# Which engine subtracts the low parts of the mixer's weights

## The chip, the core and the metric

The kernel runs on one core of a Trainium2 chip as one program. Its time is the device time of one execution in microseconds (us). The five engines of the core work side by side and each takes its instructions strictly in the order in which they were written when the program was built: TensorE (PE, matrix products), VectorE (DVE), ScalarE (ACT), GpSimd (POOL) and SyncE (SP, which here issues DMAs). What one engine needs of another it waits for on semaphores.

## The reference

The reference computes two blocks of a language model in float32 for one sequence of 512 frames with 1024 channels. The first block is a hybrid mixer followed by a convolutional feed-forward net; the second has two layers, each a mixer (stick-breaking attention with pooling, then gated linear attention) and a feed-forward net. The change lies in the first mixer. Cut to what matters there:

```
h = rms_norm(x, pre_mix_norm)
proj = h @ w_in                                   # 1024 x 6688
qkv = silu(causal_dwconv(q, k, v))                # gated delta rule, 8 heads
o_a = gdn_chunked(l2norm(q), l2norm(k), v, g, beta)   # per chunk a triangular solve,
                                                  # then a recurrence over the chunks
o_a = rms_norm(o_a) * silu(z_a)
xbc = silu(causal_dwconv(x_s, b_s, c_s))          # Mamba-2 state space, 16 heads
y = rms_norm((ssd_chunked(xbc, dt, ...) + d * x_s) * silu(z_s))
x = x + rms_norm(concat(o_a, y) @ w_out, post_mix_norm)
```

## The kernel before

All activations lie with channels on the 128 partitions and the 512 frames along the free axis. A weight matrix is read in tiles of 128 x 1024 floats. For accuracy close to float32 each weight tile and each activation is kept as two parts in a rounded format: a high part, which is a cast, and a low part, which is the original minus the high part. One product then takes three matmuls: high times high (L214), high weight times low activation (L215), low weight times high activation (L216).

A weight tile goes through `wload`: SP issues the DMA into `wr` (two buffers), ACT casts `wr` to `wh` (L202), and a subtraction makes `wl` (L205). `wh` and `wl` have four buffers each. In the first mixer (`mix1`, which sets `s.wpool = WP` at L611 and back to 0 at L1051) the subtraction of every second tile is on GpSimd and that of the others on VectorE:

```
        s.nw += 1
        e = nc.gpsimd if s.wpool and s.nw % s.wpool == 0 else nc.vector
        e.tensor_tensor(lo[:, :f], raw[:, :f], hi[:, :f], ALU.subtract)
```

`mix1` treats the eight heads of the gated delta rule in four pairs (`gdn`). For each pair, TensorE makes the products of keys (L747) and of keys with queries (L769), DVE masks and scales them, a reduction (L756) collects the diagonal blocks, which go through DRAM and back (L757, L762) to lie as the solve needs them. The solve itself is a chain of thirty small DVE instructions (L791, L792, each needing the one before), ended by two L801. After it TensorE transposes the result (`pX`, L798), two levels of block inversion follow (L812 to L836), then the recurrence over four chunks (L851 to L867), the norm (a chain L183 to L188, then L877) and a transpose into place (`pfo`, L880). In the text, a *solve* is the stretch from the second L756 of a pair to its first L801.

Beside this, projections are fed to TensorE as filling: those of the next pair of heads (L474, L479, L691 are their convolution and activation), of the gates, and of the state-space part (`xbc`). Which filling stands between which steps of the chain, and in which order each engine sees its instructions, is settled when the program is built by a scheduler, which goes by priorities and by its own estimate of how long each instruction takes. The state-space part (`ssd_prep`, `ssd_core`) transposes its inputs (`ps`, L698), scales them on DVE (L957) and GpSimd (L960, `xd`), and accumulates states (`pS`, L971) and outputs (`py`, L999; `pf`, L1022). GpSimd also makes a mask product per head (L771), some low parts of activations (L296), and issues the loads of decay rows (L677).

Of the kernel before, what the change touches and what calls it, by code (L numbers as in the profile page):

```python
# [90 lines left out]
class Prog:  # L91
# [513 lines left out]
    def mix1(s, after):  # L605
# [4 lines left out]

        s.wpool = WP  # L611
        rv = s.cp.tile([P, 64], F32, name="rv")
# [795 lines left out]
GF = [[0], [1], [2, 3], []]  # L1408
PA = 0
PB_ = 2  # L1410
WP = 2
EO = (0, 1, 0, 4, 4, 4, 1, 6, 6, 6, 6, 4, 2, 5, 5, 2, 5, 3, 5, 3)
HE = 0
FA = 13
# [153 lines left out]
```

## Time and profile before

| | |
|---|---|
| median of 3 runs | 2156.12 us (2152.16 to 2157.94) |
| the profiled execution, own time | 2157.26 us |
| its span, first to last instruction | 2155.3 us |
| TensorE busy in the span | 2083.8 us (97%) |
| VectorE busy | 1392.2 us (65%) |
| ScalarE busy | 944.4 us (44%) |
| GpSimd busy | 152.0 us (7%) |
| mean granted TensorE clock | 0.984 |

The first mixer takes about the first 620 us of the span. Busy time counts instructions from start to end, so a DVE instruction that started and was then held up counts as busy. A row of a timeline gives the start in the span, the duration, the engine, the line of the kernel, the operation, what it writes and reads, and in brackets how long the engine stood idle before it and what ended that idle time.

### The profile page before, as it was taken

Reading aid. Unit: us, or ns where it says so; the run is one execution under the profiler, and the core shown is the slowest. Engines: PE = TensorE matmul, PEld = TensorE weight load, DVE = VectorE, ACT = ScalarE, POOL = GpSimd, SP = SyncE. Lnnn points to the kernel's source line nnn. Section 1 sums busy time; section 2 is a strip of 40 time slices with the busy share of each in tenths; the row PEclk is TensorE's granted clock in tenths of the full one; section 3 lists DMA queues with packets and bytes.
Section 4 is the critical chain, followed back from the end, with each engine's and each line's share of the span. In section 5 each row is a group of like instructions: output and inputs, shape, how many; then the busy total and the mean of one; then the engine's idle time right before and its main releaser. Section 6 shows DMA issues by size and latency. Waiting matters only on the chain.

```text
span 2155.3 us, 27129 instructions
## 1 busy us (share of the span) xinstructions
PE 2083.8 (97%) x10558; PEld 1740.6 (81%) x10558; DVE 1392.2 (65%) x2353; ACT 944.4 (44%) x1557; POOL 152.0 (7%) x109
## 2 busy tenths in 40 slices
PE   8989989988999999999999999999999999999999
PEld 7777878877788888889777788888889888888887
DVE  6868666687579777227887787763243576777621
ACT  6434435356455444224765444442242434444311
POOL 1111111134000000000000100001000001000000
PEclk9999999999999999999999999999999999999999
DMA  4213131233213223332212132233322122322331
GB/s 163 96 54 97 40 98 52 69 108 98 97 51 119 98 96 96 98 101 80 67 47 66 55 121 95 97 94 97 94 81 88 59 79 68 118 98 98 95 116 64
DMA packets 60358, 189.16 MB, mean 88 GB/s; under 512 B 7901, under 2 KB 13277, under 8 KB 60230
## 3 DMA queue, kind: packets, MB, share of 16 engines
q1 hardware_dynamic: 57874, 180.75, 26.1%
q0 software_dynamic: 2032, 6.59, 0.9%
q8 instruction: 83, 1.36, 0.2%
q14 instruction: 45, 0.37, 0.0%
q10 hardware_dynamic: 324, 0.09, 0.0%
HBM read 184.99 MB, written 2.41 MB: 87 GB/s over the span
## 4 chain that ended last, share of the span: by engine, by line
PE 80%; DVE 11%; ACT 4%; DMA 2%; issue 2%; POOL 1%; SPq 0%; ACTq 0%; POOLq 0%; DVEq 0%
PE pp L214 23%; PE pp L216 23%; PE pp L215 23%; DVE qkv L479 1%; DVE wl L205 1%; DMA wr<-in_w_qkvz 1%; PE pT L812 1%; PE pz L1124 1%; PE pU L819 1%; DVE xbc L479 1%; PE pS L1367 1%; ACT wh L202 1%; PE po L1376 1%; DVE s L791 1%; DVE t L683 1%
## 5 line engine op out<-in xcount | busy, mean ns | idle before, releaser
L214 PE MATMUL pp<-a,wh 128*128 128x512 f32 (+1 forms) x2128 | 825.5, 389 | 8.5 <-ACT a L295 2.5
L215 PE MATMUL pp<-a,wh 128*128 128x512 f32 (+1 forms) x2128 | 819.7, 386 | 2.8 <-POOL a L296 2.2
L216 PE MATMUL pp<-a,wl 128*128 128x512 f32 (+1 forms) x2128 | 818.9, 385 | 3.3 <-POOL wl L205 1.7
L202 ACT CAST wh<-wr 128x1024 fp32r<-128x1024 f32 (+3 forms) x327 | 336.2, 1030 | 512.9 <-PE pp L215 370.0
L205 DVE TENSOR_TENSOR wl<-wr,wh 128x1024 fp32r<-128x1024 f32 (+2 forms) x297 | 358.1, 1206 | 235.9 <-ACT wh L202 232.2
L214 PEld LDWEIGHTS pp<-a,wh 128*128 128x128 f32 x2128 | 403.3, 190 | 92.7 <-issue 8.3
L215 PEld LDWEIGHTS pp<-a,wh 128*128 128x128 f32 x2128 | 404.0, 190 | 82.5 <-issue 4.0
L216 PEld LDWEIGHTS pp<-a,wl 128*128 128x128 f32 x2128 | 403.7, 190 | 81.5 <-DVE wl L205 2.9
L466 DVE TENSOR_TENSOR u<-pp,rb 128x512 f32<-128x512 f32 x198 | 135.6, 687 | 172.2 <-PE pp L216 170.7
L479 DVE SCALAR_TENSOR_TENSOR c<-u,pv,c 128x511 f32<-128x511 f32 (+1 forms) x264 | 196.3, 747 | 3.9
L216 PE MATMUL pp<-t,wl 128*128 128x512 f32 (+1 forms) x336 | 130.9, 389 | 0.0
L214 PE MATMUL pp<-t,wh 128*128 128x512 f32 (+1 forms) x336 | 130.7, 389 | 0.0
L215 PE MATMUL pp<-t,wh 128*128 128x512 f32 (+1 forms) x336 | 129.7, 386 | 0.0
L214 PE MATMUL pp<-wh,a 128*128 128x256 f32 (+2 forms) x384 | 112.6, 295 | 6.4 <-ACT wh L355 4.9
L215 PE MATMUL pp<-wl,a 128*128 128x256 f32 (+2 forms) x384 | 112.6, 293 | 0.0
L216 PE MATMUL pp<-wh,a 128*128 128x256 f32 (+2 forms) x384 | 112.6, 293 | 0.0
L476 ACT ACTIVATE c<-u,pv 128x512 f32<-128x512 f32 x132 | 107.5, 815 | 10.8 <-DVE u L466 10.3
L205 POOL TENSOR_TENSOR wl<-wr,wh 128x1024 fp32r<-128x1024 f32 x30 | 73.8, 2462 | 353.3 <-ACT wh L202 252.3
L499 ACT ACTIVATE c<-c 128x512 f32<-128x512 f32 x66 | 41.7, 632 | 106.7 <-DVE c L479 106.4
L214 PEld LDWEIGHTS pp<-wh,a 128*128 128x128 f32 x384 | 74.3, 194 | 8.4 <-ACT wh L355 4.9
L315 POOL TENSOR_TENSOR t<-t,t 128x512 f32<-128x512 f32 x18 | 29.4, 1635 | 727.6 <-ACT t L313 727.2
L295 ACT CAST t<-c 128x512 fp32r<-128x512 f32 x42 | 26.1, 621 | 114.9 <-DVE c L500 114.9
(343 smaller groups left out, 2353.0 us busy)
## 6 DMA issues: line engine op xcount, KB each, us to landing
wr<-in_w_up SPq DMA_DIRECT2D x132, 512.0 KB
wr<-in_w_dn SPq DMA_DIRECT2D x48, 448.0 KB
wr<-in_w_qkvz SPq DMA_DIRECT2D x32, 512.0 KB
wr<-in_w_dn SPq DMA_DIRECT2D x24, 512.0 KB
t<-gcd POOLq DMA_DIRECT2D x24, 256.0 KB, 4.4
wr<-in_w_xbc SPq DMA_DIRECT2D x12, 512.0 KB
a<-bdd SPq DMA_DIRECT2D x32, 128.0 KB
wr<-in_w_o1a SPq DMA_DIRECT2D x8, 512.0 KB
```

Source lines behind the costliest of these rows:

```text
L202: nc.scalar.copy(hi[:, :f], raw[:, :f])
L205: e.tensor_tensor(lo[:, :f], raw[:, :f], hi[:, :f], ALU.subtract)
L214: mm(out, l[0], r[0], start=first, stop=False)
L215: mm(out, l[0], r[1], start=False, stop=False)
L216: mm(out, l[1], r[0], start=False, stop=last)
L295: nc.scalar.copy(hi, src)
L315: (nc.vector if s.pool_sq or last else nc.gpsimd).tensor_tensor(s.acc, s.acc, sq, ALU.add)
L466: s.nc.vector.tensor_tensor(u, ps, rb, ALU.mult)
L476: nc.scalar.activation(c, u, AF.Identity, scale=w(taps - 1), bias=bias)
L479: nc.vector.scalar_tensor_tensor(c[:, sh:], u[:, :S - sh], w(j), c[:, sh:], ALU.mult, ALU.add)
L499: nc.scalar.activation(g, g, AF.Silu)
L683: v.tensor_scalar(r[:, c * P:(c + 1) * P], r[:, c * P:(c + 1) * P], gc3[:, c, h:h + 1], 0.0, ALU.subtract, ALU.min)
```

## The change

The constant that chooses which tiles of the first mixer go to GpSimd goes from 2 (every second) to 0 (none).

```
-WP = 2
+WP = 0
```

All else of the source stays. The scheduler, however, now has 30 instructions fewer on GpSimd and 30 more on DVE, and it lays out all engines anew for the stretch of the first mixer; after that stretch the order is as before. On GpSimd, from the program's start to the first mask products (L771), the piece of the difference reads:

```order
-L205 ISA
-L205 TENSOR_TENSOR wl_496<-wr_493,wh_495 128x1024
-L205 TENSOR_TENSOR wl_574<-wr_571,wh_573 128x1024
 L677 DMA t_610<-gcd 128x512
 L677 DMA t_612<-gcd 128x512
-L205 TENSOR_TENSOR wl_819<-wr_816,wh_818 128x1024
-L205 TENSOR_TENSOR wl_948<-wr_945,wh_947 128x1024
+L771 ISA
 L771 TENSOR_TENSOR t_610<-t_610,cmix_281 128x512
```

All subtractions are gone, and the loads of decay rows and the mask products stand behind nothing but each other. On DVE, in the middle of the first pair's solve, this stood before (`s_894`, `s_896` are the running solution and a product; `u` and `qkv` belong to a projection of the next heads):

```order
L791 TENSOR_TENSOR s_896<-a_718,s_894 128x8x12
L205 TENSOR_TENSOR wl_1103<-wr_1100,wh_1102 128x1024
L792 TENSOR_TENSOR s_894<-s_894,s_896 128x8x12
L791 TENSOR_TENSOR s_896<-a_719,s_894 128x8x11
L466 TENSOR_TENSOR u_1015<-pp_990,rb_364 128x512
L792 TENSOR_TENSOR s_894<-s_894,s_896 128x8x11
L791 TENSOR_TENSOR s_896<-a_719,s_894 128x8x10
L792 TENSOR_TENSOR s_894<-s_894,s_896 128x8x10
L791 TENSOR_TENSOR s_896<-a_719,s_894 128x8x9
```

and this stands now:

```order
L791 TENSOR_TENSOR s_896<-a_719,s_894 128x8x11
L205 TENSOR_TENSOR wl_1103<-wr_1100,wh_1102 128x1024
L792 TENSOR_TENSOR s_894<-s_894,s_896 128x8x11
L466 TENSOR_TENSOR u_1015<-pp_990,rb_364 128x512
L791 TENSOR_TENSOR s_896<-a_719,s_894 128x8x10
L205 TENSOR_TENSOR wl_1137<-wr_1134,wh_1136 128x1024
L792 TENSOR_TENSOR s_894<-s_894,s_896 128x8x10
L479 SCALAR_TENSOR_TENSOR qkv_1017<-u_1015,pv,qkv_1017 128x511
L791 TENSOR_TENSOR s_896<-a_719,s_894 128x8x9
```

The tile `wl_1137`, which GpSimd subtracted before, now stands between two links of the chain, beside `wl_1103`. On TensorE, at the start of the state-space part, this stood before (the transposes `ps`, then filling `pp`, then the states `pS`):

```order
L698 MATMUL ps_4018<-cst,xbc_3933 128x128 x4
L214 MATMUL pp_4298<-a_126,wh_4294 128x512
...
L214 MATMUL pp_4298<-a_218,wh_4294 128x512
L698 MATMUL ps_4029<-cst,xbc_3972 128x128 x4
L971 MATMUL pS_4040<-xd_4002,Bt_3982 128x128
L971 MATMUL pS_4040<-xd_4013,Bt_3982 128x128
L971 MATMUL pS_4040<-xd_4024,Bt_3982 128x128
```

and this stands now:

```order
L880 MATMUL pfo_3737<-cst,t_3735 128x128 x4
L698 MATMUL ps_3983<-cst,xbc_3777 128x128 x4
L945 MATMUL pc_3989<-xbc_3816,xbc_3777 128x128 x4
...
L698 MATMUL ps_4029<-cst,xbc_3972 128x128 x4
L214 MATMUL pp_4337<-a_218,wh_4333 128x512
L215 MATMUL pp_4337<-a_219,wh_4333 128x512
L971 MATMUL pS_4040<-xd_4002,Bt_3982 128x128
L216 MATMUL pp_4337<-a_218,wl_4334 128x512
```

Before, 39 matmuls of filling stood between the last `pfo` of the heads and the first of these transposes, and 16 between the transposes and the states; now the transposes follow `pfo` at once and the states come after two matmuls of filling.

## Rows read from the trace of the kernel before

**Rows 1.** Busy time per engine, granted clock (PEclk): the first mixer, and a half-clock stretch
```profile
0.00:620.00 620.00, 561.90 (x3260) 484.92 (x3260) 441.07 (x944) 294.15 (x650) 111.48 (x82) 0.95 0.27 88
207.80:221.50 13.70, 12.87 (x52) 11.49 (x52) 6.92 (x9) 3.76 (x6) 2.54 (x1) 0.50 0.25 78
```

**Rows 2.** TensorE's waits in the first mixer: us in total, times, longest
```profile
PE pX L798 <- DVE t L801: 22.6, 4, 8.7
PE pf L1022 <- ACT a L1019: 6.5, 2, 4.0
...
PE pfo L880 <- DVE t L877: 2.8, 3, 2.3
PE po L459 <- DVE t L455: 2.5, 1, 2.5
PE pp L215 <- POOL a L296: 2.2, 2, 1.4
...
PE pp L216 <- POOL wl L205: 1.7, 1, 1.7
```

**Rows 3.** TensorE at the transposes behind the four solves
```profile
117.44 1.11 PE L798 MATMUL pX<-cst,t 128*128 128x128 f32 x4 [6.82 <-DVE t L801]
208.59 1.11 PE L798 MATMUL pX<-cst,t 128*128 128x128 f32 x4 [4.48 <-DVE t L801]
299.06 1.12 PE L798 MATMUL pX<-cst,t 128*128 128x128 f32 x4 [8.75 <-DVE t L801]
380.93 0.66 PE L798 MATMUL pX<-cst,t 128*128 128x128 f32 x4 [2.56 <-DVE t L801]
```

**Rows 4.** The subtractions on each engine, first mixer: busy, mean ns, idle before
```profile
L205 POOL TENSOR_TENSOR wl<-wr,wh 128x1024 fp32r<-128x1024 f32 x30 | 73.8, 2462 | 353.3 <-ACT wh L202 252.3 <-PE pp L216 26.4 <-DVE s L187 25.6
L205 DVE TENSOR_TENSOR wl<-wr,wh 128x1024 fp32r<-128x1024 f32 x40 | 50.9, 1273 | 21.7 <-ACT wh L202 21.3 <-issue 0.3
```

**Rows 5.** GpSimd in the first solve
```profile
101.67 2.39 POOL L205 TENSOR_TENSOR wl<-wr,wh 128x1024 fp32r<-128x1024 f32 x1 [13.10 <-ACT wh L202]
110.15 2.35 POOL L205 TENSOR_TENSOR wl<-wr,wh 128x1024 fp32r<-128x1024 f32 x1 [6.09 <-ACT wh L202]
```

**Rows 6.** DVE in the first solve
```profile
86.92 2.19 DVE L479 SCALAR_TENSOR_TENSOR qkv<-u,pv,qkv 128x509 f32<-128x509 f32 x1
...
99.09 0.74 DVE L479 SCALAR_TENSOR_TENSOR qkv<-u,pv,qkv 128x509 f32<-128x509 f32 x1
...
101.80 2.37 DVE L791 TENSOR_TENSOR s<-a,s 128x88 f32<-128x88 f32 x1
...
110.15 0.68 DVE L466 TENSOR_TENSOR u<-pp,rb 128x512 f32<-128x512 f32 x1
110.75 1.81 DVE L791 TENSOR_TENSOR s<-a,s 128x48 f32<-128x48 f32 x1
```

**Rows 7.** DVE at other places: two norms, the third and the fourth solve
```profile
26.25 2.22 DVE L186 TENSOR_TENSOR s<-R 128x4 f32<-128x4 f32 x1
...
157.59 0.16 DVE L186 TENSOR_TENSOR s<-s 128x8 f32<-128x8 f32 x1
157.78 2.35 DVE L187 SCALAR_TENSOR_TENSOR s<-s,s 128x8 f32<-128x8 f32 x1
...
290.30 1.23 DVE L205 TENSOR_TENSOR wl<-wr,wh 128x1024 fp32r<-128x1024 f32 x1 [3.55 <-ACT wh L202]
...
366.08 0.28 DVE L791 TENSOR_TENSOR s<-a,s 128x120 f32<-128x120 f32 x1 [4.15 <-DMA a<-bdd]
...
374.23 2.42 DVE L791 TENSOR_TENSOR s<-a,s 128x48 f32<-128x48 f32 x1
```

**Rows 8.** TensorE's pace on filling, six matmuls apart
```profile
480.65 0.39 PE L214 MATMUL pp<-a,wh 128*128 128x512 f32 x1
...
482.01 0.39 PE L214 MATMUL pp<-a,wh 128*128 128x512 f32 x1
```

**Rows 9.** GpSimd before the first states
```profile
437.75 3.35 POOL L960 TENSOR_TENSOR xd<-t,s 128x384 f32<-128x384 f32 x3 [1.22 <-DVE t L957]
```

## Prediction

> **What bounds the kernel now.** Read busy time per engine for the first mixer, where alone instructions move [rows 1]: TensorE is busy 561.9 of 620 us, so 58.1 us are idle, and the granted clock averages 0.95. A stretch such as 207.8 to 221.5 us stands at 0.50, the lower level of 1.2 GHz; it began beside a TensorE wait of 4.48 us [rows 1, 3]. If TensorE sets the pace throughout, the missing 0.05 is worth 620 x 0.05 = 31 us. So at most 58.1 + 31 = 89 us are to be had from this change, and it has them only where TensorE waits less.
>
> Then read what TensorE waits for [rows 2]. Weights are not it: a low part from GpSimd held it up once, for 1.7 us. The largest item is the transpose behind the solves, 22.6 us, which falls into 6.82, 4.48, 8.75 and 2.56 us [rows 3]; then the ends of norms (`pf` 6.5, `pfo` 2.8, L459 2.5). All of these are chains of small DVE instructions.
>
> Then read why those chains are late, by laying GpSimd's timeline over DVE's. While GpSimd subtracts from 101.67 to 104.06 us, a tiny L791 that starts at 101.80 takes 2.37 us [rows 5, 6]; the same kind takes 0.28 elsewhere [rows 7]. In the subtraction that starts at 110.15 an L466, which reads one input from PSUM, takes its usual 0.68, and the L791 after it takes 1.81 [rows 5, 6]. An L479 at 86.92 takes 2.19 instead of 0.74 [rows 6], an L186 2.22 instead of 0.16, an L187 2.35 [rows 7]. So a DVE instruction with both inputs in SBUF that starts inside a GpSimd subtraction ends about when that does. Of the 30 subtractions some 22 hold one so, by 1.4 to 2.2 us.
>
> The Trainium skill (SBUF — State Buffer, Who interferes with whom) has it that an instruction of VectorE with two SBUF inputs and a GpSimd one that reads SBUF exclude each other for the whole instruction, and that one with at most one SBUF input, outside certain modes, runs beside it. The rows agree with both halves (2.37 us for L791, 0.68 for L466).
>
> **The change part by part.** *DVE's load.* It removes 30 GpSimd subtractions of 2.46 us each and adds 30 on DVE; DVE's own had a mean of 1.27, holds included, and 1.23 undisturbed [rows 4, 7]. That adds 30 x 1.23 = 36.9 us and takes away some 22 x 1.85 = 41 us of holds: DVE's load stays about level. What changes is where it falls, and the order.
>
> *The four solves.* Between the second L756 and the first L801 I count in the two orders of DVE what stands there, with 0.74 us for an L479, 0.68 for an L466, 1.23 for a subtraction, and in TensorE's order the filling matmuls between the last transposes of the inputs and `pX`. Filling has a pace of 1.36 / 6 = 0.227 us per 512-column matmul [rows 8]; 256 columns are put at half, 0.113, an estimate.
> - First: one L479, one L466 and four subtractions more, +6.34; three holds less (1.45, 2.09, 1.53 [rows 6, 7]), -5.07. Filling goes from 137 to 158 matmuls: 4.77 us more cover. Wait: 6.82 + 1.27 - 4.77 = 3.3.
> - Second: one L479, one L466, two subtractions more, +3.88; two holds like the first two, -3.54; 12 matmuls more, 2.72. Wait: 4.48 + 0.34 - 2.72 = 2.1.
> - Third: two subtractions more, one L466 fewer, +1.78; one hold like L791's, -2.09. Filling: 22 wide matmuls fewer, 56 narrow ones more, 1.4 us more. Wait: 8.75 - 0.31 - 1.4 = 7.0.
> - Fourth: after the first L791, which waits 4.15 us for its data anyway [rows 7] and so absorbs what is put before it, nine L479, one L466 and two subtractions more, +9.80; one hold (2.42 - 0.28), -2.14. Filling: 68 wide more, 63 narrow fewer, 8.3 us. Wait: 2.56 + 7.66 - 8.3 = 1.9.
>
> Together 14.3 in place of 22.6, -8.3. Each subtraction added to DVE also waits for its cast at the head of DVE's queue, and the small chain stands behind it; on GpSimd the same wait (353 us of idle time there) cost nobody anything [rows 4]. DVE's 40 had 21.7 us of idle time before them, 0.54 each [rows 4]; the worst in a solve was 3.55 [rows 7]. For the ten extra ones that is 0 to 35 us. I take the mean, 10 x 0.54 = +5.4, since these come from the same loads. Net of the solves: **-2.9**.
>
> *Other places where a hold or GpSimd itself stood right before a TensorE wait.* The first norm (L186, 2.06 us of hold) before L459; the first head norm (L187, 2.19) before `pfo`; the low part that TensorE awaited, 2.46 against 1.23, so 1.23; activations' low parts on GpSimd (2.2 us of wait [rows 2]) behind a subtraction of 2.46 in GpSimd's queue, so 2.2; the two waits `pf`, of 4.0 and 2.5 us [rows 2]: the first keeps 3.7, since it loses a hold of 2.1 but also 8 matmuls of filling (1.8), the second gains 17 matmuls (3.9 us) and goes. Sum 2.06 + 2.19 + 1.23 + 2.2 + 2.8 = 10.5: **-10.5**. Bounds: 0, if another input is late next, and 10.5; I take the upper one, because after these holds nothing but one or two instructions stands before TensorE.
>
> *What comes new.* At the state-space part the cover of 39 and 16 matmuls is gone. The states then wait for DVE's scaling (some 0.7 us) and four L960, 3.35 / 3 = 1.12 us each [rows 9], so up to 5.2 us; the transposes and two to nine matmuls hide part. Twice that gives 0 to 10; I take the middle, **+5**.
>
> *Clock.* Idle time changes by -2.9 - 10.5 + 5 = -8.4 of 58.1, that is 14%; the same share of 31 us gives **-4.4** (bounds 0 and -10).
>
> The sum: -2.9 - 10.5 + 5 - 4.4 = -12.8. The profiled execution took 2157.26, 1.96 more than its span; it would take 2144.5. It lies 1.1 above the median of the runs, so the median comes out at about **2143 us**.
>
> **Rivals.** *DVE's queue stalls in the solves (slower).* One mechanism: a subtraction at the head of DVE's queue whose weight tile is still in transfer holds up the chain of L791. For it: 3.55 us at 290.30 [rows 7], and six subtractions now stand inside the first solve. Against it: the mean is 0.54. It decides from the point where the ten extra ones wait 0.54 + 12.8 / 10 = 1.8 us each; at 3 us each they cost 30 in place of 5.4, and the time is 2143 + 25 = 2168. If only TensorE's share of that is felt, 2160.
>
> The Trainium skill (Perfetto Trace Analysis, Optimizing Scalar/DVE Operations) says that with VectorE saturated, shifting some work to GpSimd may make sense, though their shared port may undo it. By the first half the change loses; here DVE is busy 441 of 620 us [rows 1], which does not look saturated over the stretch but nearly is within a solve.
>
> *No change.* The new order gives away elsewhere what the holds return: the two pieces -10.5 and +5 come out equal, the solves at 0, the time 2153 to 2158. For it: the chain of heads now ends 78 filling matmuls (18 us) later in TensorE's order, so the state-space part has less filling left. Against it: the total of filling is the same and no new work is on TensorE.
>
> *A larger gain.* The solves lose all of the 8.3 and nothing waits at casts, the states wait no longer than before: -8.3 - 10.5 = -18.8, with the clock's share (32% of 31, 10) -29: 2127.
>
> **How the numbers follow.** A difference of 0.3%, 6.5 us, is about what a measurement of this kernel can tell from none. Forecast (2130 to 2149) 0.53, larger gain 0.10, no change 0.17, stall 0.20. Faster 0.63, same 0.17, slower 0.20. The range goes from 2124 to 2166: it leaves out some 0.05 below and 0.12 above; the forecast's own is 2130 to 2149.
>
> **What would show it.** No DVE instruction with inputs in SBUF longer than its usual time, but for those beside L771, L296 and L960; the waits before `pX` at about 3, 2, 7 and 2 us; those of L459 and `pfo` under 1 us; new waits before `pS`; idle time of DVE before L205 of about 38 us over 70. The forecast is wrong if TensorE's idle time in the first 620 us does not fall below 54 us, or if DVE's waits for casts exceed 60 us.

## The result and the profile after

The changed kernel takes 2120.39 us (median of 4 runs, 2119.10 to 2123.84), beside 2157.03 us (4 runs) of the kernel before on the same chip: a ratio of 0.983, 95% interval 0.981 to 0.985. That is 36.6 us less. The prediction had 12.8 us less (2143) and a range that ended at 2124, so it had the direction and was almost three times too small.

The profiled execution, the slowest of the four, has a span of 2122.1 us, 33.2 below the 2155.3 of before. TensorE is busy 2078.7 us of it (page, part 1) against 2083.8; so 28.1 us of the 33.2 are idle time that is gone. The other 5.1 us are shorter matmuls, as many as before (10558), at a mean granted clock of 0.989 in place of 0.984; they are put down to the clock. The first window answers to [rows 1], in its columns; the second is the longest stretch at the lower level, 1.2 GHz:

```profile
0.00:620.00 620.00, 587.84 (x3476) 506.64 (x3476) 458.27 (x1044) 309.34 (x678) 39.88 (x52) 0.97 0.28 91
113.10:126.80 13.70, 13.01 (x53) 12.02 (x54) 4.58 (x9) 3.43 (x5) 0.00 (x0) 0.50 0.16 45
```

In the same 620 us TensorE is idle for 32.2 instead of 58.1 us and has done 216 matmuls more. The half-clock stretch begins beside the first transposes behind a solve, the longest of these waits that is left. What TensorE waits for in the first mixer, which now ends some 34 us earlier (answers to [rows 2]; us in total, times, longest):

```profile
PE pX L798 <- DVE t L801: 8.8, 3, 5.3
...
PE pp L215 <- DVE a L296: 2.6, 1, 2.6
...
PE pS L971 <- POOL xd L960: 1.5, 3, 0.7
PE pp L215 <- POOL a L296: 1.5, 2, 0.9
...
PE pp L216 <- DVE wl L205: 1.0, 2, 0.5
PE pf L1022 <- ACT a L1019: 0.9, 2, 0.5
...
PE ps L698 <- ACT qkv L691: 0.7, 1, 0.7
PE po L459 <- DVE t L455: 0.5, 1, 0.5
PE pfo L880 <- DVE t L877: 0.2, 1, 0.2
```

The transposes behind the solves go from 22.6 to 8.8 us and every end of a norm falls to under 1 us. Items that the prediction had not read stood in the same view of before. `py` and the two waits of the state-space part's transposes (`Bt`, `xbc`) are gone now, the one behind L691 is at 0.7. The other two lines belong beside the waits for low parts above, of weights and of activations:

```profile
PE py L999 <- DVE t L986: 3.3, 3, 2.4
PE ps L698 <- ACT qkv L691: 3.1, 1, 3.1
...
PE ps L698 <- ACT Bt L941: 1.2, 1, 1.2
PE pp L216 <- DVE wl L205: 0.9, 2, 0.6
PE ps L698 <- ACT xbc L923: 0.7, 1, 0.7
PE pp L215 <- DVE a L296: 0.6, 1, 0.6
```

The four transposes of the kernel after, answers to [rows 3] (6.82, 4.48, 8.75, 2.56 us there):

```profile
113.79 1.11 PE L798 MATMUL pX<-cst,t 128*128 128x128 f32 x4 [5.35 <-DVE t L801]
207.54 0.65 PE L798 MATMUL pX<-cst,t 128*128 128x128 f32 x4 [3.08 <-DVE t L801]
286.13 0.66 PE L798 MATMUL pX<-cst,t 128*128 128x128 f32 x4 [0.34 <-DVE t L801]
373.58 0.60 PE L798 MATMUL pX<-cst,t 128*128 128x128 f32 x4
```

All 70 subtractions are on DVE, and the time that DVE stood at the head of its queue waiting for their casts is 9.1 us where [rows 4] had 21.3 us for 40 (columns as there, window 0 to 590 us):

```profile
L205 DVE TENSOR_TENSOR wl<-wr,wh 128x1024 fp32r<-128x1024 f32 x70 | 85.8, 1227 | 9.5 <-ACT wh L202 9.1 <-issue 0.3
```

In the first solve the links of the chain keep their usual length, with a subtraction between two of them; compare 2.37 and 1.81 us in [rows 6]:

```profile
105.68 0.21 DVE L791 TENSOR_TENSOR s<-a,s 128x56 f32<-128x56 f32 x1
105.80 1.22 DVE L205 TENSOR_TENSOR wl<-wr,wh 128x1024 fp32r<-128x1024 f32 x1
106.94 0.21 DVE L792 TENSOR_TENSOR s<-s,s 128x56 f32<-128x56 f32 x1
```

A held DVE instruction is left only where GpSimd still has work, as beside the low parts of the heads' outputs. First GpSimd, two instructions in a row, then DVE, where an L186 takes 0.15 us undisturbed:

```profile
466.97 3.93 POOL L296 TENSOR_TENSOR a<-a,a 128x512 fp32r<-128x512 f32 x2 [4.53 <-ACT a L295]
```
```profile
465.25 0.15 DVE L186 TENSOR_TENSOR s<-s 128x4 f32<-128x4 f32 x1
...
467.39 1.23 DVE L186 TENSOR_TENSOR s<-s 128x4 f32<-128x4 f32 x1
```

### The profile page after: what moved, and what is told of

It reads as the page before. It is cut to its first block, busy times and chain, and to the rows that moved or that the text cites. A ratio compares the mean times of both kernels' runs of the same rounds, so it can differ in the third digit from the quotient of the medians.

```text
span 2122.1 us, 27151 instructions
## 1 busy us (share of the span) xinstructions
PE 2078.7 (98%) x10558; PEld 1734.2 (82%) x10558; DVE 1380.9 (65%) x2383; ACT 943.2 (44%) x1555; POOL 80.4 (4%) x79
## 4 chain that ended last, share of the span: by engine, by line
PE 82%; DVE 8%; ACT 4%; DMA 3%; issue 1%; POOL 0%; SPq 0%; ACTq 0%; DVEq 0%; POOLq 0%
PE pp L214 24%; PE pp L215 24%; PE pp L216 24%; DVE wl L205 2%; DMA wr<-in_w_qkvz 1%; DVE qkv L479 1%; PE pz L1124 1%; PE pU L819 1%; PE pT L812 1%; PE pS L1367 1%; ACT wh L202 1%; PE po L1376 1%; DMA a<-bdd 1%; ACT s L712 1%; PE py L999 0%
## 5 line engine op out<-in xcount | busy, mean ns | idle before, releaser
L202 ACT CAST wh<-wr 128x1024 fp32r<-128x1024 f32 (+3 forms) x327 | 336.6, 1031 | 513.7 <-PE pp L215 385.6
L205 DVE TENSOR_TENSOR wl<-wr,wh 128x1024 fp32r<-128x1024 f32 (+3 forms) x327 | 393.2, 1203 | 222.4 <-ACT wh L202 218.7
L479 DVE SCALAR_TENSOR_TENSOR c<-u,pv,c 128x511 f32<-128x511 f32 (+1 forms) x264 | 196.5, 748 | 3.9
L214 PEld LDWEIGHTS pp<-wh,a 128*128 128x128 f32 x384 | 74.1, 194 | 9.7 <-ACT wh L355 4.8
L295 ACT CAST t<-c 128x512 fp32r<-128x512 f32 x42 | 26.1, 621 | 114.9 <-DVE c L500 114.9
L216 PEld LDWEIGHTS pp<-wh,a 128*128 128x128 f32 x384 | 74.3, 194 | 1.5 <-issue 1.4
L215 PEld LDWEIGHTS pp<-wl,a 128*128 128x128 f32 x384 | 74.2, 193 | 1.6 <-issue 1.2
```

Of the source, the lines that this page charges most:

```text
L202: nc.scalar.copy(hi[:, :f], raw[:, :f])
L214: mm(out, l[0], r[0], start=first, stop=False)
L215: mm(out, l[0], r[1], start=False, stop=False)
L216: mm(out, l[1], r[0], start=False, stop=last)
L295: nc.scalar.copy(hi, src)
L479: nc.vector.scalar_tensor_tensor(c[:, sh:], u[:, :S - sh], w(j), c[:, sh:], ALU.mult, ALU.add)
```

## Experiments

The change does two things at once: it moves 30 subtractions to another engine, and it makes the scheduler lay out every engine anew. To take these apart, several kernels fix an order. A function at the end of the program ties each instruction of an engine to the one that shall stand before it there, without any wait; the order is a list of numbers, one row per engine. Its core, with cuts marked by dots:

```
+def pin(tc, blob):
...
+    cur = tc.nc.cur_bb.bb.instructions
+    by = {i.name: i for i in cur}
...
+    for row in rows:
...
+            if prev is not None:
+                tc.add_manual_dep(i, prev.name, ..., reason="pin")
+            prev = i
...
+        pin(tc, ORDER)
```

"The order of before" and "the order of after" are the orders on TensorE, ScalarE, SyncE and DVE through the first mixer.

**The means itself: before, with its own order fixed** (edit: `pin` and the list, nothing else).

> The kernel before with its own order fixed by the same means as in the other runs of fixed order; no engine's order differs and no wait is added. Every theory expects the time of before, 2152 to 2162; a difference would be what fixing an order costs by itself.

Measured: 2154.45 us, 0.9999 of before (0.998 to 1.002). Fixing this order costs nothing that can be measured, so the runs below can be compared with those that the scheduler laid out.

**The engine alone: the order of before, all subtractions on DVE.** The 30 stand on DVE where GpSimd made them in time.

```
-WP = 2
+WP = 0
+        pin(tc, ORDER)
```

> All instructions of TensorE, ScalarE, SyncE and VectorE in the order of the kernel before; only the 30 subtractions that GpSimd made are on VectorE, each at the place at which GpSimd had made it, but never ahead of an earlier tile's. Theory H (the holds): what GpSimd's subtractions held up on VectorE is the gain, whatever the order; 25 to 35 us below before, 2122 to 2132. Rival O (the order): the gain comes from the new layout (filling moved in front of the solves, weights loaded at other points); within 8 us of before, 2149 to 2160, since 30 more instructions of 1.2 us stand in VectorE's queue. Idle time of TensorE in the first mixer (52.7 us before up to its last norm): H about 30, O about 50.

**The order alone: the order of after, every second subtraction on GpSimd.** GpSimd's own order is free.

```
+        pin(tc, ORDER)
```

> All instructions of TensorE, ScalarE, SyncE and VectorE in the order of the changed kernel, but every second tile of the first mixer is subtracted on GpSimd again. H: the holds are back, 2145 to 2165. O: the order keeps most of the gain, 2118 to 2130.

**Neither: the order of before, the 30 left out.** The third product of those tiles reads the high part, so the output lacks 30 low parts. Where nothing is subtracted, a name is used up all the same, so that the later instructions keep the names by which the list orders them.

```
+            lo = ... if not (s.wpool and (s.nw + 1) % s.wpool == 0) else (..., hi)[2]
...
-        e.tensor_tensor(lo[:, :f], raw[:, :f], hi[:, :f], ALU.subtract)
+        e = nc.vector
+        nc.get_next_instruction_name() if lo is hi else e.tensor_tensor(lo[:, :f], raw[:, :f], hi[:, :f], ALU.subtract)
...
+        pin(tc, ORDER)
```

> The order of the kernel before on all engines, and the 30 subtractions of GpSimd left out: the third product of these tiles reads the high part in place of a low part, so the result lacks those low parts. Against o_before_dve it prices the 30 subtractions on VectorE, against before those on GpSimd. H: 28 to 40 us below before (2117 to 2129), and 0 to 8 below o_before_dve, since VectorE is no bottleneck once nothing holds it. O: within 8 us of before. A third view, that a subtraction costs about its own time wherever it stands in a chain, has it 25 us or more below o_before_dve.

**The same in the order of after.**

> The order of after on every engine with the 30 subtractions left out (the third product of those tiles reads the high part instead, so their low parts are missing from the output). In the order of before the 30 cost 44 us on GpSimd and 21.5 on DVE by the time. If the new layout hides them (its waits at casts are short, its solves have more filling), they cost less here: 0 to 12 us, so 2108 to 2121 against 2120 after. If they cost in any order what they cost in that of before, 0.72 us each, 2095 to 2102.

The five together, as median and ratio to before (half-width of the interval 0.002 to 0.003):

| | 30 on GpSimd | 30 on DVE | 30 left out |
|---|---|---|---|
| order of before | 2154.45, 0.9999 | 2135.27, 0.9909 | 2113.78, 0.9805 |
| order of after | 2151.87, 0.9973 | 2120.39, 0.9829 | 2114.36, 0.9809 |

Read across, the engine is worth 0.9 to 1.4% in either order; read down, the order is worth 0.3% with GpSimd at work, 0.8% with DVE, and nothing when there is nothing to subtract. So neither theory is right alone: the engine is the larger part, some 20 us in the order of before (22.5 by the medians of one comparison, 19.5 by the ratios) and 31 in that of after, and the new order pays its most only once GpSimd is out of the way. What 30 subtractions cost is the difference to the last column: in the order of before 44 us of the run's time on GpSimd (2157.82, before in that comparison, less 2113.78) and 21.5 on DVE; in that of after 37.5 and 4 to 6 (2151.87, and 2120.39 or in a second comparison 2118.31, each less 2114.36). By the ratios the two costs on GpSimd are 42 and 35 us. My expectation that holds would put the run without subtractions within 8 us of the run with them on DVE was wrong: in the order of before each still costs 0.72 us, and the third view, that a subtraction costs about its own time (25 us or more), came nearer with 21.5. In the new order the cost is small. The intervals of the two ratios there overlap, but on the one chip that ran both, every run of the kernel after (2116.86 to 2121.34) lies above every run without the 30 (2111.13 to 2116.36), so it isn't nothing.

The waits show which part is whose. The profiled executions of the two crossed runs were the fastest of their runs (2128.20 and 2145.97 us), so their waits may be a little short. The order of before with all on DVE, TensorE and then DVE:

```profile
PE pX L798 <- DVE t L801: 16.5, 4, 6.2
...
PE pf L1022 <- ACT a L1019: 4.3, 2, 2.9
...
PE py L999 <- DVE t L986: 0.2, 1, 0.2
```
```profile
DVE wl L205 <- ACT wh L202: 21.8, 20, 8.1
```

The order of after with half on GpSimd, TensorE:

```profile
PE pX L798 <- DVE t L801: 13.6, 4, 6.6
PE py L999 <- DVE t L986: 7.1, 3, 4.0
...
PE pfo L880 <- DVE t L877: 4.5, 4, 1.3
```

and the order of after without the 30:

```profile
PE pX L798 <- DVE t L801: 7.8, 2, 5.2
```

DVE's waits for casts stay at 21.8 us in the order of before, for 70 subtractions in place of 40 (21.3): most of the added ones find their casts done. They fall to 9.1 in the new order. The larger part of that fall is one wait near the end of the mixer, 9.6 us in the kernel before and 8.1 in this run, which the new order doesn't have. And the wait behind the solves falls by 6 us by the engine alone, by 9 by the order alone, by 14 by both. Yet by the time the order alone gives only 6 us: with GpSimd at work it has longer waits at other places, 7.1 us before `py` in place of 3.3 and 4.5 before `pfo` in place of 2.8.

**Holds, or a tile that is ready late?** GpSimd takes 2.46 us for a tile against 1.23, so besides holding DVE it frees `wr` and hands over the tile later. The next run shortens the holds and keeps the rest: the order of before, each GpSimd subtraction in four pieces.

```
-        e.tensor_tensor(lo[:, :f], raw[:, :f], hi[:, :f], ALU.subtract)
+        for c in (range(0, f, 256) if e is nc.gpsimd else (None,)):
+            r = slice(0, f) if c is None else slice(c, c + 256)
+            e.tensor_tensor(lo[:, r], raw[:, r], hi[:, r], ALU.subtract)
...
+        pin(tc, ORDER)
```

> The order of before on every engine, and the same 30 subtractions on GpSimd, but each cut into four of 256 columns. GpSimd's work, its place in the chain from load to matmul and the two buffers of wr stay as they are; only the longest time for which one of its instructions can keep a DVE instruction waiting falls from about 2.4 to about 0.6 us. Theory 'holds': what GpSimd costs is that a DVE instruction of a chain waits for the end of the GpSimd instruction, some 22 times 1.85 us; cut in four, about 0.4 is left of each, and most of the 22 us between before and the run with the subtractions on DVE in the same order (2135) comes back: 2132 to 2146, with DVE's small instructions no longer than about 0.9 us. Rival 'slow tile' (a tile from GpSimd is ready later and its wr buffer free later, 2.46 against 1.23 us): nothing changes, 2150 to 2165, although the small instructions are short. If GpSimd goes on holding DVE through all four quarters, the instructions stay at 2.2 to 2.4 us and the time at 2150 to 2165, and the run decides nothing.

Measured: 2153.27 us, 1.000 of before (0.998 to 1.002). By its words this is the rival's number, but the trace does not bear the rival out. In the first solve, GpSimd and DVE (line numbers are two higher here: L793 and L794 are L791 and L792):

```profile
104.75 2.90 POOL L207 TENSOR_TENSOR wl<-wr,wh 128x256 fp32r<-128x256 f32 x4 [10.80 <-ACT wh L202]
```
```profile
104.60 0.25 DVE L794 TENSOR_TENSOR s<-s,s 128x96 f32<-128x96 f32 x1
104.89 0.72 DVE L793 TENSOR_TENSOR s<-a,s 128x88 f32<-128x88 f32 x1
105.52 0.68 DVE L468 TENSOR_TENSOR u<-pp,rb 128x512 f32<-128x512 f32 x1
106.12 0.23 DVE L794 TENSOR_TENSOR s<-s,s 128x88 f32<-128x88 f32 x1
106.39 0.67 DVE L793 TENSOR_TENSOR s<-a,s 128x80 f32<-128x80 f32 x1
107.09 0.66 DVE L794 TENSOR_TENSOR s<-s,s 128x80 f32<-128x80 f32 x1
```

Between two pieces of GpSimd's, DVE gets one instruction through and the next is held again, by about 0.4 us; three are held in place of one, by 1.3 us together. Count as held a DVE instruction that overlaps a subtraction on GpSimd and takes over 0.4 us more than the median of its kind in all the runs. Over the mixer, 52 are held by 25 us in all (the longest 0.58), where the unsplit kernel with the same order fixed has 23 and 44 us (the longest 2.22); in the four solves the fall is only from 15 to 10 us. In return GpSimd's tiles take 103.1 us in place of 73.6. A piece takes 0.73 us even beside an idle DVE, more than a quarter of 2.4, and GpSimd is held in turn: beside DVE instructions in close succession one piece took 3.20. Shorter holds and slower tiles changed together, so this run decides nothing; the next one keeps the holds and takes the late buffer away.

**Holds without the late buffer: the order of before, all subtractions on DVE, and GpSimd busy with nothing needed.**

```
-        e = nc.gpsimd if s.wpool and s.nw % s.wpool == 0 else nc.vector
-        e.tensor_tensor(lo[:, :f], raw[:, :f], hi[:, :f], ALU.subtract)
+        nc.vector.tensor_tensor(lo[:, :f], raw[:, :f], hi[:, :f], ALU.subtract)
+        if s.wpool and s.nw % s.wpool == 0:
+            one = s.c("ones").unsqueeze(1).to_broadcast([P, 8, P])
+            lo3 = lo.rearrange("p (a b) -> p a b", b=P)
+            nc.gpsimd.tensor_tensor(lo3, lo3.bitcast(F32), one, ALU.mult)
...
+        pin(tc, ORDER)
```

> The order of before with the 30 subtractions on DVE (2135 as a run of its own, 0.9909 of before), and in addition 30 instructions on GpSimd that do no needed work: behind each of those subtractions GpSimd multiplies the finished low part by one in place, 128x1024, some 2.4 us. So GpSimd is as busy as in before and stands beside DVE's chains again, but the buffer of wr is free as soon as DVE has subtracted, 1.23 us after the cast. The low part is ready later than in either run; TensorE's waits for it in the profile show whether that costs anything. Theory 'holds': DVE's small instructions are held again for up to 2.2 us each, some 20 of them, and the 22 us come back: 2150 to 2162. Rival 'slow tile' (what GpSimd cost was wr's buffer free 1.2 us later, and so every second weight load): holds are in the trace, but the time stays within 5 us of 2135. In between, 2140 to 2150, both have a share.

Measured: 2175.65 us, 1.009 of before (1.006 to 1.012), so 40 us above the run without this extra work, more than any theory had. GpSimd, DVE (L795 is L792) and TensorE's waits:

```profile
107.22 2.40 POOL L208 TENSOR_TENSOR wl<-wl,cst 128x1024 fp32r<-128x1024 f32 x1 [11.41 <-DVE wl L204]
```
```profile
107.15 0.68 DVE L469 TENSOR_TENSOR u<-pp,rb 128x512 f32<-128x512 f32 x1
107.75 1.97 DVE L795 TENSOR_TENSOR s<-s,s 128x88 f32<-128x88 f32 x1
109.75 0.24 DVE L794 TENSOR_TENSOR s<-a,s 128x80 f32<-128x80 f32 x1
```
```profile
PE pX L801 <- DVE t L804: 27.6, 4, 9.7
...
PE pp L219 <- POOL wl L208: 4.6, 1, 4.6
PE pp L218 <- POOL a L299: 4.1, 2, 3.3
```

25 DVE instructions are held here by 43 us in all, counted as above. Some 8 us of the 40 are not holds: TensorE waits 4.6 us for a low part that is now ready later still, and 3.2 us more for other low parts behind it in GpSimd's queue (4.1 against 0.9). The other 32 us don't fit the rival, which had this run within 5 us of 2135: `wr` is freed by DVE, as in that run. So a microsecond of hold costs some 0.75 us of the run here (32 / 43), and the rival falls as the main cause. The theory of the holds had expected only 22 us. It took what moving the subtractions gave for the price of the holds, but that gain is net of the 21.5 us that the subtractions cost on DVE. In before 23 instructions are held by 42 us; at the same rate, an estimate, that is 32 of the 44 us that GpSimd's 30 subtractions cost. What the other 12 are, late buffers among them, stays open.

**The two halves of the change.** The first half moves 18 subtractions, the second 12.

```
-        s.wpool = WP
+        s.wpool = 0
...
+        s.wpool = WP
```

> The subtractions are on DVE in the first mixer's part of the heads (the first 51 of its 70 weight tiles) and still alternate from the state-space part on; the scheduler lays out all engines anew. This divides the gain of 37 us by place. View 'price per subtraction' (each one that leaves GpSimd gives back the same, 30 to 37 us over 30 of them, wherever it stands): about 20 of the 30 move here, so 2129 to 2138, and this and the other half add up to the whole within 6 us. View 'layout' (much of the gain is that the chains and the filling happen to fall better, so a half made by its own need not give half): the two halves miss the sum by more than 10 us, and one of them may give nothing (over 2150).

```
+        s.wpool = 0
```

> The other half: GpSimd subtracts every second tile in the part of the heads, as before, and none from the state-space part on, where the change left TensorE's waits before pf (6.5 us before, 0.9 after), py (3.3, 0) and ps (3.1, 0.7). Price per subtraction: about 10 of 30 move, so 2143 to 2149. Layout: anything from 2130 to 2160, with the waits before pX as in before (about 20 us) in either case.

Measured: the heads alone 2131.45 us (0.989, 0.986 to 0.991), the state-space part alone 2138.71 (0.993, 0.990 to 0.995), before 2157.28. That is 25.8 and 18.6 us, 1.4 and 1.6 us per subtraction: every place gives some, as the price per subtraction has it. But the second half gave 4 us more than that price allowed. The sum of 44.4 is 7.8 above the whole by the medians, between what the two views expected, and by the ratios 3.4 (1.13% and 0.74% against 1.71%), within the 6 us of the price; so the two halves don't tell the views apart. The scheduler lays each out differently; in the second the waits before `pX` are as in before:

```profile
PE pX L798 <- DVE t L801: 20.8, 4, 8.0
```

**The rest of GpSimd's work.** After, with the four low parts of the heads' outputs on DVE as well, then with the mask products too.

```
-PA = 0
+PA = 2
```

> The kernel after with the last GpSimd subtractions of the first mixer, the four low parts of the heads' outputs (L296, 1.5 to 2.3 us each, beside which DVE's L184 to L187 are held for about 1.1 us each), on DVE too. If holds and GpSimd's slowness are the cause and go on being it, TensorE's waits for L296 on GpSimd (1.5 us) go, and about four holds: 1 to 5 us faster than after, 2115 to 2120. If what helps is only that there is less to do around the solves, this is worth nothing, since no solve is near: 2119 to 2124, DVE taking 0.68 us more for each of the four in the same stretch where the norms run.

```
-                nc.gpsimd.tensor_tensor(v3(PT[i]), v3(PT[i]), tri_b, ALU.mult)
+                v.tensor_tensor(v3(PT[i]), v3(PT[i]), tri_b, ALU.mult)
```

> The same, and the eight mask products (L771, 1.29 us each on GpSimd) on DVE too, where each takes about 0.7 us. They stand in the products of keys and queries just ahead of the solves. By the price of a GpSimd subtraction against one on DVE (1.47 against 0.72 us of the whole time for each in the order of before) this gives 8 x 0.75 = 6 us less than the run before it. By DVE's load (the instructions of a solve wait in one queue, and GpSimd's mask products end long before anyone needs them) it costs 0 to 6 us more.

**The kernel after once more.**

> The kernel after once more, for its distance to the run with the heads' low parts on DVE as well (2115.7, against before 0.9813): the same 2118 to 2124, that is 0.982 to 0.984 of before, and so 3 to 6 us above that run if that one's gain is real; if it is not, 2114 to 2118.

Measured: 2115.69 (0.981, 0.979 to 0.984), 2121.53 (0.985, 0.982 to 0.987), and the kernel after again 2118.31 (0.983, 0.981 to 0.986). The intervals overlap, so moving the heads' low parts may give 3 us or nothing. Moving the masks gives nothing more: the median is 5.8 us above the run before it, on the side of DVE's load. In the first of them TensorE's wait for these low parts is as long as after's 2.6 + 1.5 and has only changed hands:

```profile
PE pp L215 <- DVE a L296: 4.3, 2, 4.1
```

No version was found that is told apart from the kernel after as faster, but for those that leave work out.

## Why the prediction was too small

- **The mechanism held.** GpSimd's subtractions held up DVE's small instructions, and this bounded TensorE's waits. Held instructions are left only beside GpSimd's other work; the run with unneeded GpSimd work brings the loss back and more. The Trainium skill (SBUF — State Buffer, SBUF: two separate sides) has it that of a DVE instruction with two SBUF inputs and a GpSimd one that reads SBUF, whichever starts first has the shared pair of ports for the whole instruction. By that, 1.97 us for a link that takes 0.24 agrees, and so does the one instruction that slips between two of GpSimd's quarters.
- **The solves: -2.9 predicted, -13.8 in the trace.** The step that failed is the term "each subtraction added to DVE also waits for its cast", +5.4, taken as ten times the mean of 0.54. Inside the four solves DVE waited 5.4 us for casts before (0.86, 1.00, 3.55 and none) and 3.55 after (0.85, 1.66, none and 1.05), so the term came out at -1.9. The mean was no price for a solve: 9.62 of its 21.7 us are one wait some 180 us after the last solve:

```profile
567.88 1.23 DVE L205 TENSOR_TENSOR wl<-wr,wh 128x1024 fp32r<-128x1024 f32 x1 [9.62 <-ACT wh L202]
```

The waits at `pX` miss even the -8.3 ahead of that term by another 5.5 us, a balance of errors. The third came out 6.7 us below its forecast (0.34 for 7.0) and the fourth 1.9 below, the first and second 2.0 and 1.0 above. From second L756 to first L801 the four solves take 31.9, 25.1, 24.2 and 23.4 us before and 35.2, 26.1, 20.2 and 28.4 after, 5.3 longer in sum, where the prediction's counts and casts made it 14.4 longer. The third became 4.0 us shorter, where 0.3 was counted: its 3.55 us at the cast [rows 7] went with its hold. The filling counted from the order came out right in two: wait saved plus lengthening is 4.8 us for the first solve (4.77 predicted) and 2.4 for the second (2.72). In the third it is 4.4 in place of 1.4. The first became 3.3 us longer where 1.3 was counted, with a wait of 4.03 us in it that the prediction didn't have. ScalarE stands at a cast whose tile is still in transfer, its L474 stands behind that, and at the head of DVE's queue, ahead of the chain, an L479 waits for L474 (0.32 us before):

```profile
92.42 1.05 ACT L202 CAST wh<-wr 128x1024 fp32r<-128x1024 f32 x1 [5.71 <-DMA wr<-in_w_qkvz]
93.37 0.63 ACT L691 ACTIVATE qkv<-qkv 128x512 f32<-128x512 f32 x1
93.90 0.71 ACT L474 ACTIVATE qkv<-u,pv 128x512 f32<-128x512 f32 x1
```
```profile
94.64 0.75 DVE L479 SCALAR_TENSOR_TENSOR qkv<-u,pv,qkv 128x511 f32<-128x511 f32 x1 [4.03 <-ACT qkv L474]
```
- **Ends of norms and GpSimd's own lateness: -10.5 predicted, -10.5 found, by luck.** L459 2.5 to 0.5 and `pfo` 2.8 to 0.2 came as said, and the awaited low parts of weights went from 1.7 + 0.9 to 1.0, where 1.23 less was said. But `pf` gave 5.6 in place of 2.8, and the low parts of activations, said to give 2.2, took 1.3 more: 2.2 + 0.6 became 1.5 + 2.6.
- **New waits at the state-space part: +5 predicted, -4.1 found.** This is the second step that failed. The new waits before `pS` are there, 1.5 us in three, up by 1.1 from 0.4. But the waits that stood there before went, and the prediction had never read them: `py` -3.3 us, and 1.9 us before the transposes of the inputs (1.2 + 0.7). The engine alone is what took `py` away: it is at 0.2 us in the order of before with all subtractions on DVE, and at 7.1 in the order of after with GpSimd at work. I had looked at what the loss of cover exposes and not at what was exposed already. Another 2.4 us went outside all terms, at the first transposes of the heads (`ps` behind L691, 3.1 to 0.7).
- **Clock: -4.4 predicted, -5.1 found**, but for an idle time that fell 28.1 us and not 8.4, so the agreement is luck. The rule of equal shares, 31 us for 58, was too steep.
- **The rivals.** Stalls of DVE's queue at casts did not come: 0.13 us per subtraction after, where 1.8 was its point of decision. One stall of that kind came by way of ScalarE's queue, the 4.03 us above. The larger gain, with all casts ready and no new waits, was the nearest (2127), and even it left out `py`, `ps` and the rest of `pf`. Of the idle time that the sum missed, 28.1 - 8.4 = 19.7 us, 10.9 lie in the solves, 9.1 at the state-space part and 2.4 at the heads' start. Some 2 us of new small waits elsewhere go the other way, the largest at a cast of ScalarE (`wh` L202, 0.2 before and 1.9 now).
- **The skill's advice.** That shifting work to GpSimd may make sense when VectorE is saturated, though for the shared port it might not help (the Trainium skill, Perfetto Trace Analysis, Optimizing Scalar/DVE Operations), agrees here in its second half. With 30 instructions more on DVE, its busy time over the whole span, holds included, went down from 1392.2 to 1380.9 us, and the kernel got faster. (In the first 620 us it rose from 441.07 [rows 1] to 458.27, but there that window takes in some 34 us of later work.)

## What to carry to other kernels

Work on a slow engine that nobody waits for is not free when it holds up the engine that carries the chains: read it by the instructions it stretches, all of them, and not only those that stand right before a wait of TensorE. Where filling hides the chains, price an added instruction from the stretch's cover and the casts' readiness and not from a mean wait, and when the cover goes down at one place, read all waits of that place, also those that can only fall. A run that leaves the work out shows about what placing it better can still give: here 2114 in both orders, so the 30 subtractions on DVE in the new order are already within 4 to 6 us of free.

## What the runs showed of the hardware

- Unneeded work on GpSimd beside DVE's chains, 30 instructions of about 2.5 us on SBUF data, cost 40 us of the run, though TensorE waited for its results only once, for 4.6 us.
- Cutting a GpSimd instruction in four did not free DVE: one DVE instruction with two SBUF inputs passed between two pieces, each further one waited for a piece, and GpSimd's own tile took 3.4 in place of 2.5 us (103.1 / 30 and 73.6 / 30).
- The hold goes both ways: a piece that takes 0.73 us beside an idle DVE took up to 3.20 beside DVE instructions in close succession.
- The same 30 subtractions cost 0.72 us each of the run on DVE in one order and at most 0.2 in another (6.0 / 30).
